# Weight splits of whole 128x2048 buffers, memory tokens kept in DRAM, and four sets of seven block products in the first feed-forward part

## The chip, the cores and the metric

The kernel runs on one core of one Trainium2 chip. The metric is the device time of one execution in microseconds (us). Before the change it is 1260.77 us, the median of 3 runs (1260.51 to 1260.87).

## What is computed

A trunk of two layers on 256 tokens of width 1024, all in fp32, batch 1. Memory is 256 further tokens, normalised once per layer with its own gain.

```python
for i in range(2):
    h = h + 0.5 * swiglu(rmsnorm(h, ffn1_norm[i]), ffn1_w_gate[i], ffn1_w_up[i], ffn1_w_down[i])
    hn = rmsnorm(h, mix_norm[i])
    h = h + (diff_attention(hn, ...) if i == 0 else ssd_mixer(hn, ...))
    h = h + memory_cross_attention(rmsnorm(h, xa_norm[i]), mem, xa_mem_norm[i], xa_w_q[i], xa_w_kv[i], xa_w_o[i])
    h = h + 0.5 * swiglu(rmsnorm(h, ffn2_norm[i]), ffn2_w_gate[i], ffn2_w_up[i], ffn2_w_down[i])
return rmsnorm(h, final_norm)

def swiglu(h, w_gate, w_up, w_down):      # hidden width 2816
    return (silu(h @ w_gate) * (h @ w_up)) @ w_down
```

## The kernel before

**Products.** TensorE (PE) multiplies fp32r operands. To keep fp32 accuracy, every operand is split into a rounded part (hi) and the rest (lo), and a product is three matmuls: hi by hi (line 262), hi by lo of the weights (263), lo by hi (264), function `mm3`.

**Weights.** A weight block of 4 x 128 rows and 512 columns is loaded with one DMA of 1 MB, issued on SyncE (SP), into a buffer of 128x2048 out of a pool of 8 (`wp`, tile `w`). A piece (`Gran`, lines 205 to 226) is half a block, 128x1024. It is split by a CAST on ScalarE (ACT, line 224, tile `whi`) and a subtract on VectorE (DVE, line 225, tile `wlo`), into two tiles of 128x1024 out of a pool of 4 (`hp`). `use` (line 236) splits two pieces (`AHEAD`) ahead of the one that PE multiplies. In the code a list of units says in which order the pieces come. `run_units` writes the first two units (gate 0 and up 0 of the first feed-forward part, FFN) by hand on PE, DVE, ACT and SP; the rest is put in order by a scheduler.

**FFN.** The hidden width 2816 is five blocks of 512 (0 to 4) and half a block (5). A block of gate and up by the plain way is 2 x 8 k-blocks x 2 halves of the tokens = 32 products of 128x512. `seven` (line 352) makes one of them in 28 products: the two weight matrices, cut into four blocks b11, b21 (of up), b12, b22 (of gate), are combined with sums of the activations so that seven block products with four products each do. Its operands are x1 = b11 + b12 (a sum on DVE, line 203), x2 = x1 + b22 (DVE too, into x1's buffer, after x1 has been split), x3 = b12 + b22 and x4 = x2 + b21 (accumulating DMAs on GpSimd, line 199). The order in a set is x1, b11, x2, b22, x3, b21, x4. The sums of activations are made on DVE (`sraw`, line 481, from `y`, line 560) and split as `s_hi` (ACT, 485) and `s_lo` (DVE, 486). Results in PSUM, tile `seven`, are copied and combined as `p` (lines 823 to 841).

**Hosts.** Ordinary pieces, of up 0, of the half block (`gateup`), and of the down projection (`out`), are put between the pieces of the sets: `share` places `counts[c][i]` of them ahead of the i-th piece of set c. A host piece is four products for each k-block pair: 2 k-blocks x 2 halves of the tokens. In the first FFN block 0 is done by hand, and half block 5 and block 1 by the plain way (`stream`), as hosts; blocks 2 to 4 are sets. In the other three FFNs blocks 1 to 4 are sets.

**Memory.** `mem_prep` transposes the normalised memory on PE and keeps it in SBUF as eight tiles `mem` of 128x256. The cross-attention reads them in `prep` (scaled and split as `mh`, `ml`, for the keys) and `mix` (scaled as `my`, for the values as sums).

Of the kernel before, what the change touches and what calls it, by code (L numbers as in the profile page):

```python
# [57 lines left out]
def trunk(ctx, tc, a, out):  # L58
# [146 lines left out]
    class Gran:  # L205


        def __init__(self, k0, nk, *parts, eng=None):
            self.k0, self.nk, self.parts, self.eng = k0, nk, parts, eng or nc.vector
            self.hi = None  # L210

        def split(self):
# [2 lines left out]
            hi = hp.tile([P, 1024], F32R, name="whi", tag="hi")
            lo = hp.tile([P, 1024], F32R, name="wlo", tag="lo")
            ncol = sum(n for _, _, n in self.parts)
            self.hi, self.lo = (t[:, :self.nk * ncol].rearrange("p (k c) -> p k c", c=ncol) for t in (hi, lo))
            o = 0
            for w, c0, n in self.parts:  # L220
                w.load()
                src = w.t[:, self.k0 - w.k0:self.k0 - w.k0 + self.nk, c0:c0 + n]
# [1 line left out]
                nc.scalar.copy(hv, src)  # L224
                self.eng.tensor_tensor(self.lo[:, :, o:o + n], src, hv.bitcast(F32), op=ALU.subtract)  # L225
# [462 lines left out]
    def mem_prep():  # L688
# [12 lines left out]
        def turn(j):  # L701
            ps = small_ps("tin")
            for t in range(2):
                nc.tensor.transpose(ps[:, t * P:(t + 1) * P], mnat[t][j // 4][:, (j % 4) * P:(j % 4 + 1) * P], ident)
            nc.scalar.copy(memt[j], ps[:, :S])
        for j in range(KT):
            pipe.after(6.0 + 1.0 * j, lambda j=j: turn(j))
# [349 lines left out]
    class MemKV:  # L1057


        def __init__(self, l):  # L1060
# [20 lines left out]

        def prep(self):
            self.x.clear()
            for j in range(KT):
                if j % 2 == 0:
                    mh, ml = slot("mh", F32R), slot("ml", F32R)
                xh, xl = (m[:, j % 2 * S:(j % 2 + 1) * S] for m in (mh, ml))
                split_act(xh, xl, memt[j], self.g[:, j:j + 1])
                self.x.append((xh, xl))
# [587 lines left out]
```

## Time and profile before

| what | value |
|---|---|
| median of 3 runs | 1260.77 us |
| the profiled execution | 1260.69 us |
| its span | 1258.9 us |
| busy: PE, DVE, ACT, POOL | 1248.6, 1056.7, 878.0, 161.7 us |
| granted PE clock, mean | 0.998 |
| splits of 128x1024 | 520 |
| weight reads from HBM and rest | 269.79 MB, mean 214 GB/s |

The span is what the profiler saw; 1.8 us of the execution lie around it. Busy times of engines overlap. PE's own busy time is modelled, so its waits are read from the distance between the starts of matmuls. In a row of the timeline the first column is the start in us from the span's beginning, the second the duration (of all that the row groups, "x2" is two of them), and in brackets stands how long the engine had been idle and what released it. A group's row ends with the busy time, the mean in ns of one, and the idle time ahead of it.

### The profile page before, as it was taken

Reading aid. Unit: us, or ns where it says so; the run is one execution under the profiler, and the core shown is the slowest. Engines: PE = TensorE matmul, PEld = TensorE weight load, DVE = VectorE, ACT = ScalarE, POOL = GpSimd, SP = SyncE. Lnnn points to the kernel's source line nnn. Section 1 sums busy time; section 2 is a strip of 40 time slices with the busy share of each in tenths; the row PEclk is TensorE's granted clock in tenths of the full one; section 3 lists DMA queues with packets and bytes.
Section 4 is the critical chain, followed back from the end, with each engine's and each line's share of the span. In section 5 each row is a group of like instructions: output and inputs, shape, how many; then the busy total and the mean of one; then the engine's idle time right before and its main releaser. Section 6 shows DMA issues by size and latency. Waiting matters only on the chain.

```text
span 1258.9 us, 18179 instructions
## 1 busy us (share of the span) xinstructions
PE 1248.6 (99%) x6751; PEld 1070.7 (85%) x6751; DVE 1056.7 (84%) x1451; ACT 878.0 (70%) x1395; POOL 161.7 (13%) x139
## 2 busy tenths in 40 slices
PE   9999999999999999999999999999999999999997
PEld 6887888788998888888888889999998898888886
DVE  6988867887787998988898976788899887899886
ACT  6676764676676876767776756777777775877673
POOL 1101002201101011101111000022232100011100
PEclk9999999999999999999999999999999999999999
DMA  9979975345776698985899966665634786489961
GB/s 335 281 205 283 319 240 183 118 144 150 209 226 168 168 264 270 267 268 167 219 273 265 289 228 214 205 186 168 201 135 135 189 245 177 159 235 276 261 215 34
DMA packets 158316, 269.79 MB, mean 214 GB/s; under 512 B 6890, under 2 KB 43411, under 8 KB 158227
## 3 DMA queue, kind: packets, MB, share of 16 engines
q1 hardware_dynamic: 137744, 229.75, 53.6%
q0 software_dynamic: 19744, 38.28, 17.8%
q8 instruction: 53, 0.87, 0.3%
q10 hardware_dynamic: 738, 0.59, 0.1%
q14 instruction: 37, 0.30, 0.1%
HBM read 267.52 MB, written 1.08 MB: 213 GB/s over the span
## 4 chain that ended last, share of the span: by engine, by line
PE 91%; DVE 4%; DMA 2%; ACT 1%; issue 1%; POOL 0%; POOLq 0%; DVEq 0%; ACTq 0%
PE out L263 9%; PE out L264 8%; PE out L262 8%; PE seven L264 8%; PE seven L263 8%; PE seven L262 8%; DVE wlo L225 2%; PE xs L264 2%; PE xs L262 1%; PE xs L263 1%; DMA w<-in_ffn_w_gate_dram 1%; PE up L263 1%; PE up L264 1%; PE up L262 1%; PE htp L854 1%; PE mk L262 1%
## 5 line engine op out<-in xcount | busy, mean ns | idle before, releaser
L225 DVE TENSOR_TENSOR wlo<-w,whi 128x1024 fp32r<-128x1024 f32 (+2 forms) x532 | 641.0, 1219 | 136.2 <-ACT whi L224 126.7
L224 ACT CAST whi<-w 128x1024 fp32r<-128x1024 f32 (+2 forms) x534 | 552.3, 1040 | 261.9 <-PE out L264 102.5
L262 PE MATMUL out<-whi,hid_hi 128*128 128x512 f32 x336 | 131.4, 394 | 0.5 <-ACT whi L224 0.5
L263 PE MATMUL out<-wlo,hid_hi 128*128 128x512 f32 x336 | 131.3, 391 | 0.4 <-DVE wlo L225 0.3
L264 PE MATMUL out<-whi,hid_lo 128*128 128x512 f32 x336 | 131.0, 390 | 0.0
L262 PE MATMUL seven<-whi,s_hi 128*128 128x512 f32 x272 | 107.7, 396 | 0.4 <-ACT p L823 0.4
L263 PE MATMUL seven<-wlo,s_hi 128*128 128x512 f32 x272 | 106.1, 390 | 0.0
L264 PE MATMUL seven<-whi,s_lo 128*128 128x512 f32 x272 | 106.1, 390 | 0.0
L203 DVE TENSOR_TENSOR w<-w 128x2048 f32<-128x2048 f32 x32 | 73.2, 2286 | 5.7 <-DMA w<-in_ffn_w_gate_dram 5.6
L199 POOL DMA_DIRECT2D w<-in_ffn_w_up_dram x30 | 36.5, 1241 | 310.5 <-DVE wlo L225 273.7
L263 PEld LDWEIGHTS out<-wlo,hid_hi 128*128 128x128 f32 x336 | 63.2, 188 | 14.7 <-DVE wlo L225 2.1
L262 PEld LDWEIGHTS out<-whi,hid_hi 128*128 128x128 f32 x336 | 63.0, 188 | 13.3 <-ACT whi L224 0.8
L264 PEld LDWEIGHTS out<-whi,hid_lo 128*128 128x128 f32 x336 | 63.1, 188 | 13.2
L262 PE MATMUL seven<-whi,xh 128*128 128x512 f32 x180 | 70.1, 389 | 0.0
L264 PE MATMUL seven<-whi,xl 128*128 128x512 f32 x180 | 70.0, 389 | 0.0
L263 PE MATMUL seven<-wlo,xh 128*128 128x512 f32 x180 | 70.0, 389 | 0.0
L199 POOL DMA_DIRECT2D w<-in_ffn_w_gate_dram x30 | 36.9, 1467 | 221.7 <-DVE w L203 76.2
L264 PEld LDWEIGHTS seven<-whi,s_lo 128*128 128x128 f32 x272 | 51.1, 188 | 10.8
L262 PEld LDWEIGHTS seven<-whi,s_hi 128*128 128x128 f32 x272 | 51.1, 188 | 10.5 <-ACT p L823 0.8
L263 PEld LDWEIGHTS seven<-wlo,s_hi 128*128 128x128 f32 x272 | 51.1, 188 | 9.7
L262 PEld LDWEIGHTS seven<-whi,xh 128*128 128x128 f32 x180 | 33.8, 188 | 7.1
L263 PEld LDWEIGHTS seven<-wlo,xh 128*128 128x128 f32 x180 | 33.8, 188 | 7.1
(398 smaller groups left out, 3018.4 us busy)
## 6 DMA issues: line engine op xcount, KB each, us to landing
w<-in_ffn_w_up_dram SPq DMA_DIRECT2D x40, 1024.0 KB, 7.2
w<-in_ffn_w_down_dram SPq DMA_DIRECT2D x40, 1024.0 KB, 8.6
w<-in_ffn_w_gate_dram SPq DMA_DIRECT2D x38, 1024.0 KB, 7.1
w<-in_ssd_w_in_dram SPq DMA_DIRECT2D x24, 1024.0 KB, 5.4
w<-in_xa_w_kv_dram SPq DMA_DIRECT2D x16, 1024.0 KB, 5.1
w<-in_ffn_w_gate_dram POOLq DMA_DIRECT2D x30, 512.0 KB, 9.1
w<-in_ffn_w_up_dram POOLq DMA_DIRECT2D x30, 512.0 KB, 7.4
w<-in_da_w_in_dram SPq DMA_DIRECT2D x12, 1024.0 KB, 5.2
```

The costliest lines, as they stand in the source:

```text
L199: nc.gpsimd.dma_start(self.t[:, k:k + 2, :], w.src[r0:r0 + 2 * P, w.c0:w.c0 + w.n] .rearrange("(k p) c -> p k c", p=P), accum_op=ALU.add)
L203: nc.vector.tensor_tensor(self.t, self.l.t, w.t, op=ALU.add)
L224: nc.scalar.copy(hv, src)
L225: self.eng.tensor_tensor(self.lo[:, :, o:o + n], src, hv.bitcast(F32), op=ALU.subtract)
L262: nc.tensor.matmul(o, lhsT=lh, rhs=rh, start=start, stop=False, skip_group_check=onto)
L263: nc.tensor.matmul(o, lhsT=lh, rhs=rl, start=False, stop=False, skip_group_check=onto)
L264: nc.tensor.matmul(o, lhsT=ll, rhs=rh, start=False, stop=stop, skip_group_check=onto)
L854: nc.tensor.transpose(tp[:, j, t * P:(t + 1) * P], us[t][:, (i + j) * P:(i + j + 1) * P], ident)
```

## The change

Four things are changed.

1. Splits. Two neighbouring pieces of one weight block (k-blocks 0 and 1, 2 and 3 of a buffer, 512 columns) are now split together: one CAST and one subtract of 128x2048. A new class `Group` decides which pieces belong together; other pieces are still split one by one, into halves of a tile. `hp` has 3 tiles of 128x2048 instead of 4 of 128x1024.
2. Memory. The transposed memory lies in DRAM. Four tiles `mt` of 128x512 are written from ACT's queue, and each `prep` and `mix` first fetches four tiles of 256 KB back, on ACT's queue too, and works some 4 to 5 us later by the code's own plan.
3. The weight pool `wp` has 7 buffers instead of 8.
4. The first FFN makes block 1 as a fourth set of seven, and `counts` are even numbers everywhere, so that the two pieces of a block stay together.

```diff
-    wp = ctx.enter_context(tc.tile_pool(name="wp", bufs=8))
-    hp = ctx.enter_context(tc.tile_pool(name="hp", bufs=4))
+    wp = ctx.enter_context(tc.tile_pool(name="wp", bufs=7))
+    hp = ctx.enter_context(tc.tile_pool(name="hp", bufs=3))
...
+    class Group:
...
+        def take(self, g, unit):
+            a = self.gs[-1]
+            if len(self.gs) == 1 and a.whole(g):
+                self.merged = True
...
+        def split(self, g):
+            if self.t is None:
+                self.t = [hp.tile([P, 2048], F32R, name=n, tag=n) for n in ("whi", "wlo")]
+            if self.merged:
...
+                src = w.t[:, a.k0 - w.k0:a.k0 - w.k0 + 4, :]
+                nc.scalar.copy(hi, src)
+                nc.vector.tensor_tensor(lo, src, hi.bitcast(F32), op=ALU.subtract)
...
-    memt = [const.tile([P, S], F32, name=f"mem{j}") for j in range(KT)]
+    memt = dram.tile([P, KT * S], F32, name="memt")
...
+            mt = slot("mt")
+            nc.scalar.copy(v2(mt), ps)
+            nc.scalar.dma_start(memt[:, 512 * i:512 * i + 512], mt)
...
-        five, six = [1, 0, 1, 0, 2, 0, 1], [1, 1, 1, 0, 2, 0, 1]
...
-            n = half + stream([(wg, 512, 512)], norm, "gate", gate_fin(1)) + stream([(wu, 512, 512)], norm, "up", up_fin(1))
-            counts = {2: [5, 1, 1, 0, 2, 1, 1], 3: [1, 1, 1, 1, 2, 1, 1], 4: [1, 1, 1, 0, 2, 1, 1]}
+            n = half
+            counts = {1: [0, 0, 2, 0, 2, 0, 0], 2: [2, 0, 2, 0, 2, 0, 0], 3: [0, 0, 2, 0, 2, 0, 0], 4: [0, 0, 2, 0, 2, 0, 0]}
...
-            counts = {1: six, 2: five, 3: six, 4: five}
+            counts = {c: [2, 0, 2, 0, 2, 0, 0] for c in (1, 2, 3)}
+            counts[4] = [0, 0, 2, 0, 2, 0, 0]
...
+        def fetch(self):
+            y = [slot("my") for _ in range(KT // 2)]
+            for p in range(KT // 2):
+                nc.scalar.dma_start(y[p], memt[:, 512 * p:512 * p + 512])
+            return y
...
         def mix(self):
-            y = [slot("my") for _ in range(KT // 2)]
+            y = self.fetch()
...
-                pipe.after(1.4 * p, lambda p=p: full(p))
-            combine(y, self.s, [7.0 + 1.6 * i for i in range(8)])
+                pipe.after(5.0 + 1.4 * p, lambda p=p: full(p))
+            combine(y, self.s, [12.0 + 1.6 * i for i in range(8)])
...
         def prep(self):
             self.x.clear()
...
+            y = self.fetch()
...
+            for p in range(KT // 2):
+                pipe.after(4.0 + 1.0 * p, lambda p=p: cut(p))
```

How the order of the instructions moves. First DVE at the start, from the first up block on; each name is a tile (`wlo` the lo part of weights, `y` and `sraw` activations, `w<-w` the sum of two weight buffers). Before:

```order
L225 TENSOR_TENSOR wlo<-w,whi 128x1024 x2
L560 TENSOR_TENSOR y<-xh,xl 128x256 x2
L225 TENSOR_TENSOR wlo<-w,whi 128x1024
L560 TENSOR_TENSOR y<-xh,xl 128x256 x2
L225 TENSOR_TENSOR wlo<-w,whi 128x1024
L560 TENSOR_TENSOR y<-xh,xl 128x256 x4
L1268 TENSOR_SCALAR dskh<-vec 128x32
L225 TENSOR_TENSOR wlo<-w,whi 128x1024
L481 TENSOR_TENSOR sraw<-y 128x256 x2
L486 TENSOR_TENSOR s_lo<-sraw,s_hi 128x512
```

And now, at the same place on DVE:

```order
L253 TENSOR_TENSOR wlo<-w,whi 128x2048
L605 TENSOR_TENSOR y<-xh,xl 128x256 x2
L253 TENSOR_TENSOR wlo<-w,whi 128x2048
L605 TENSOR_TENSOR y<-xh,xl 128x256 x6
L1328 TENSOR_SCALAR dskh<-vec 128x32
L203 TENSOR_TENSOR w<-w 128x2048
L253 TENSOR_TENSOR wlo<-w,whi 128x2048
L526 TENSOR_TENSOR sraw<-y 128x256 x2
L203 TENSOR_TENSOR w<-w 128x2048
L531 TENSOR_TENSOR s_lo<-sraw,s_hi 128x512
```

The two subtracts of up 0 that each served half a buffer are one; the gateup split that stood ahead of `sraw` has been replaced by the sum x1 and its split, and the sum x2 stands ahead of `s_lo`. On PE, at the end of up 0 (`pcol` are two small transposes of parameters), before:

```order
L263 MATMUL up<-wlo,xh 128x512
L264 MATMUL up<-whi,xl 128x512
L673 MATMUL pcol<-ident,rows_99 128x128 x2
L262 MATMUL gateup<-whi,xh 128x512
L263 MATMUL gateup<-wlo,xh 128x512
L264 MATMUL gateup<-whi,xl 128x512
```

And now on PE:

```order
L308 MATMUL up<-wlo,xh 128x512
L309 MATMUL up<-whi,xl 128x512
L718 MATMUL pcol<-ident,rows_99 128x128 x2
L307 MATMUL seven<-whi,s_hi 128x512
L308 MATMUL seven<-wlo,s_hi 128x512
L307 MATMUL seven<-whi,xh 128x512
L309 MATMUL seven<-whi,s_lo 128x512
```

PE goes from up 0 straight to the first set, with b11's first product (`whi,xh`) slipped in ahead of the first matmul that needs `s_lo`. Last, DVE in the first FFN where one set ends and the next begins (`p` are results of a set, the sums `w<-w` x1 or x2, `hid_lo` the hidden activations). Before, between the third and the fourth block:

```order
L841 SCALAR_TENSOR_TENSOR p_1133<-seven,rcol,p_1133 128x512
L225 TENSOR_TENSOR wlo<-w,whi 128x1024 x3
L841 SCALAR_TENSOR_TENSOR p_1010<-seven,rcol,p_1010 128x512
L225 TENSOR_TENSOR wlo<-w,whi 128x1024
L203 TENSOR_TENSOR w<-w 128x2048
L225 TENSOR_TENSOR wlo<-w,whi 128x1024
```

And now, between the second and the third:

```order
L890 SCALAR_TENSOR_TENSOR p_894<-seven,rcol,p_894 128x512
L253 TENSOR_TENSOR wlo<-w,whi 128x2048
L890 SCALAR_TENSOR_TENSOR p_802<-seven,rcol,p_802 128x512
L766 TENSOR_TENSOR lampr<-lqk 128x128
L203 TENSOR_TENSOR w<-w 128x2048
L767 TENSOR_REDUCE lam<-lampr 128x2
L253 TENSOR_TENSOR wlo<-w,whi 128x2048 x2
```

The sum x2 (`w<-w`) stands behind the split of the new set's b11 and ahead of the split of the first host, and both splits are whole buffers.

More of the change, by code (lines that the diff above doesn't have):

```diff
@@ L210, in __init__, with size, whole @@
             self.hi = None
-        def split(self):
-            if self.hi is not None:
+        def size(self):
+            return self.nk * sum(n for _, _, n in self.parts)
+        def whole(self, other):
+            w, c0, n = self.parts[0]
+            return (self.parts == other.parts and len(self.parts) == 1 and (c0, n) == (0, 512)
+                    and self.nk == other.nk == 2 and other.k0 == self.k0 + 2)
+        def split(self):
+            if self.hi is None:
+                self.group.split(self)
@@ new lines, in trunk, with __init__ @@
+    class Group:
+        def __init__(self, g):
+            self.gs, self.n = [g], g.size()
+            self.merged = False
+            self.t = None
+        def take(self, g, unit):
+            a = self.gs[-1]
+            if len(self.gs) == 1 and a.whole(g):
+                self.merged = True
+            elif unit != a.unit or self.merged or self.n + g.size() > 2048 or a.parts[0][2] == g.parts[0][2] == 512 and a.nk > 1:
+                return False
+            self.gs.append(g)
+            self.n += g.size()
+            return True
+        def split(self, g):
+            if self.t is None:
+                self.t = [hp.tile([P, 2048], F32R, name=n, tag=n) for n in ("whi", "wlo")]
+            if self.merged:
+                a, b = self.gs
+                w = a.parts[0][0]
+                w.load()
+                hi, lo = (t.rearrange("p (k c) -> p k c", c=512) for t in self.t)
+                src = w.t[:, a.k0 - w.k0:a.k0 - w.k0 + 4, :]
+                nc.scalar.copy(hi, src)
+                nc.vector.tensor_tensor(lo, src, hi.bitcast(F32), op=ALU.subtract)
+                for x, k in ((a, 0), (b, 2)):
+                    x.hi, x.lo = hi[:, k:k + 2, :], lo[:, k:k + 2, :]
@@ L214, in split @@
                 return
[L215 to L218, printed above, removed]
+            ncol = sum(n for _, _, n in g.parts)
+            o = sum(x.size() for x in self.gs[:self.gs.index(g)])
+            g.hi, g.lo = (t[:, o:o + g.size()].rearrange("p (k c) -> p k c", c=ncol) for t in self.t)
@@ L219, in split @@
             o = 0
-            for w, c0, n in self.parts:
+            for w, c0, n in g.parts:
                 w.load()
-                src = w.t[:, self.k0 - w.k0:self.k0 - w.k0 + self.nk, c0:c0 + n]
-                hv = self.hi[:, :, o:o + n]
+                src = w.t[:, g.k0 - w.k0:g.k0 - w.k0 + g.nk, c0:c0 + n]
+                hv = g.hi[:, :, o:o + n]
                 nc.scalar.copy(hv, src)
-                self.eng.tensor_tensor(self.lo[:, :, o:o + n], src, hv.bitcast(F32), op=ALU.subtract)
+                g.eng.tensor_tensor(g.lo[:, :, o:o + n], src, hv.bitcast(F32), op=ALU.subtract)
@@ L243, in run_units @@
     def run_units():
-        for gs, _ in units:
+        for i, (gs, _) in enumerate(units):
             for g in gs:
-                g.at = len(grans)
+                g.at, g.unit = len(grans), i
+                if not grans or not grans[-1].group.take(g, i):
+                    g.group = Group(g)
+                else:
+                    g.group = grans[-1].group
                 grans.append(g)
@@ L699, in mem_prep, with turn @@
                 nc.scalar.activation(mnat[t][c], mnat[t][c], AF.Copy, scale=mcol[:, t:t + 1])
[L701 to L707, printed above, removed]
+        def turn(i):
+            ps = v2(small_ps("tin"))
+            for j in (2 * i, 2 * i + 1):
+                for t in range(2):
+                    nc.tensor.transpose(ps[:, j % 2, t * P:(t + 1) * P], mnat[t][j // 4][:, (j % 4) * P:(j % 4 + 1) * P],
+                                        ident)
+            mt = slot("mt")
+            nc.scalar.copy(v2(mt), ps)
+            nc.scalar.dma_start(memt[:, 512 * i:512 * i + 512], mt)
+        for i in range(KT // 2):
+            pipe.after(6.0 + 2.0 * i, lambda i=i: turn(i))
     def mem_stage():
@@ L1083, in prep, with cut @@
             self.x.clear()
[L1084 to L1089, printed above, removed]
+            y = self.fetch()
+            def cut(p):
+                mh, ml = slot("mh", F32R), slot("ml", F32R)
+                for j in range(2):
+                    k = 2 * p + j
+                    xh, xl = v2(mh)[:, j, :], v2(ml)[:, j, :]
+                    split_act(xh, xl, v2(y[p])[:, j, :], self.g[:, k:k + 1])
+                    self.x.append((xh, xl))
+            for p in range(KT // 2):
+                pipe.after(4.0 + 1.0 * p, lambda p=p: cut(p))
         def k_units(self, then=None, cs=(0, 2)):
```

2 lines of the change are left out of this document (1 added, 1 removed).

## The prediction, made before the changed kernel was timed

> **What bounds the kernel now.** I read the page first: the busy times, the slices and the chain that ended last.
>
> ```profile
> span 1258.9 us, 18179 instructions
> PE 1248.6 (99%) x6751; PEld 1070.7 (85%) x6751; DVE 1056.7 (84%) x1451; ACT 878.0 (70%) x1395; POOL 161.7 (13%) x139
> PE   9999999999999999999999999999999999999997
> DVE  6988867887787998988898976788899887899886
> DMA  9979975345776698985899966665634786489961
> PE 91%; DVE 4%; DMA 2%; ACT 1%; issue 1%; POOL 0%; POOLq 0%; DVEq 0%; ACTq 0%
> PE out L263 9%; PE out L264 8%; PE out L262 8%; PE seven L264 8%; PE seven L263 8%; PE seven L262 8%; DVE wlo L225 2%; PE xs L264 2%; PE xs L262 1%; PE xs L263 1%; DMA w<-in_ffn_w_gate_dram 1%; PE up L263 1%; PE up L264 1%; PE up L262 1%; P
> ```
>
> PE is 99% busy and carries 91% of the chain. So the time is the number of matmuls, and whatever makes PE wait. DVE has 84%, and its share of the chain (4%) lies mostly in the first feed-forward part (FFN): its tenths are highest in the slices 2 to 4, and DMA is full in the slices 1 and 2 (31.5 us each). Next the groups, for the price of a split, and four stretches of the timeline.
>
> ```profile
> L225 DVE TENSOR_TENSOR wlo<-w,whi 128x1024 fp32r<-128x1024 f32 x520 | 633.9, 1233 | 131.0 <-ACT whi L224 121.6 <-DMA E<-scr 1.6
> L224 ACT CAST whi<-w 128x1024 fp32r<-128x1024 f32 x520 | 544.7, 1053 | 260.9 <-PE out L264 102.5 <-PE seven L264 43.3 <-PE gateup L264 15.9
> L203 DVE TENSOR_TENSOR w<-w 128x2048 f32<-128x2048 f32 x32 | 73.2, 2286 | 5.7 <-DMA w<-in_ffn_w_gate_dram 5.6
> ```
>
> A 128x1024 subtract takes 1233 ns; the one DVE operation on a whole buffer, the sum of two weight blocks, takes 2286. A whole-buffer subtract has the sum's shape (three fp32 operands of 128x2048), so I price it at 2.29 us. PE around the start of the first up block (columns: start, duration, both in us):
>
> ```profile
> 19.25 0.39 PE L262 MATMUL up<-whi,xh 128*128 128x512 f32 x1
> 19.76 0.50 PE L263 MATMUL up<-wlo,xh 128*128 128x512 f32 x1
> ...
> 30.32 0.40 PE L264 MATMUL up<-whi,xl 128*128 128x512 f32 x1
> 30.55 0.38 PE L673 MATMUL pcol<-ident,rows 128*128 128x128 f32 x2
> 30.69 0.47 PE L262 MATMUL gateup<-whi,xh 128*128 128x512 f32 x1
> 31.01 0.39 PE L263 MATMUL gateup<-wlo,xh 128*128 128x512 f32 x1
> 31.24 0.40 PE L264 MATMUL gateup<-whi,xl 128*128 128x512 f32 x1
> ```
>
> Matmuls overlap, so what counts is start to start: 31.24 less 31.01 is 0.23, and the 46 steps from 19.76 to 30.32 make 0.23 each. A product (hi by hi, hi by lo, lo by hi) is three of these, 0.69 us.
>
> **The matmuls saved.** The hidden block 1 of the first FFN was 32 products (gate and up, 16 each) and becomes a set of seven pieces with four products each, 28. That is 12 matmuls by 0.23: **-2.76 us**, on PE itself. This term is certain.
>
> **The first up block, cut whole.** ACT and DVE there:
>
> ```profile
> 17.41 3.89 ACT L224 CAST whi<-w 128x1024 fp32r<-128x1024 f32 x4
> ...
> 18.48 2.45 DVE L225 TENSOR_TENSOR wlo<-w,whi 128x1024 fp32r<-128x1024 f32 x2 [0.58 <-ACT whi L224]
> 20.86 0.84 DVE L560 TENSOR_TENSOR y<-xh,xl 128x256 f32<-128x256 f32 x2
> ```
>
> Four casts take 3.89, so a whole buffer (two of them) takes some 1.95: from 17.41 to 19.4. The subtract can only then begin, and ends at 19.4 + 2.29 = 21.7. Before, the first half was through at 19.7 and PE's second up matmul started at 19.76. Now it starts at 21.7: **+1.94 us**. Nothing hides it, since the order on PE, ACT and DVE at that place stays and PE has no other work. The lower bound would be 0.97 (a cast of twice the size at the price of one), the upper 2.3.
>
> [...]
>
> **The first set of seven, right behind up 0.** Before, the gateup pieces stood there, which need only one split each. Now the first product needs the sum x1 of two buffers, its split, and a mixed activation (s). The rows for the parts:
>
> ```profile
> 27.13 0.75 DVE L481 TENSOR_TENSOR sraw<-y 128x256 f32<-128x256 f32 x2
> 28.56 0.69 DVE L486 TENSOR_TENSOR s_lo<-sraw,s_hi 128x512 fp32r<-128x512 f32 x1 [0.69 <-ACT s_hi L485]
> ...
> 27.91 0.62 ACT L485 CAST s_hi<-sraw 128x512 fp32r<-128x512 f32 x1 [2.28 <-DVE sraw L481]
> ...
> 23.41 1.06 ACT L224 CAST whi<-w 128x1024 fp32r<-128x1024 f32 x1 [2.11 <-DMA w<-in_ffn_w_up_dram]
> 24.36 1.27 ACT L787 ACTIVATE gs<-gate,rcol 128x512 f32<-128x512 f32 x2
> ...
> GB/s 392 385 381 388 388 392 362 319 295 268 324 349 353 354 360 347 347 346 349 360 370 388 378 381 381 392 385 395 388 378 388 388 392 385 378 395 388 388 385 378
> ```
>
> The last line is the DMA rate from 13 to 36 us, some 385 GB/s at its end, so a buffer of 1 MB follows the one before by 2.7 us. The first buffer behind up 0 landed at 23.4 (ACT waited for it), the second then at 26.1 to 26.3. I walk DVE in its new order. The subtract of up's second buffer 22.5 to 24.7; six operations y at 0.35 and dskh to 26.9; sum x1 to 29.1 (both buffers are there); ACT's cast to 31.1; the subtract to 33.4; sraw to 34.1; s_hi on ACT (behind the cast of b11, which ends at 34.4) to 34.9. PE has ended up 0 at 30.55 + 1.94 = 32.5 and the two small pcol at 32.65, and waits to 34.9: 2.25. DVE goes on with the sum x2 (2.2, to 36.3) and only then s_lo, to 36.95: PE waits some 1.45 for its third kind of matmul. The subtract of b11 comes behind s work and gs, at 41.7: 1.15. The first gateup piece: 0.45. Together **+5.30 us**. The bounds: 0.75 (only the wait for x1's own split, 33.4 less 32.65), and 5.3 with another 2.3 if one more whole operation is late.
>
> **A stall of before that should go.** PE in the first FFN at 94 to 97 us:
>
> ```profile
> 94.05 0.61 PE L262 MATMUL out<-whi,hid_hi 128*128 128x512 f32 x2
> 95.02 0.49 PE L262 MATMUL seven<-whi,s_hi 128*128 128x512 f32 x1 [0.35 <-ACT p L823]
> 95.96 0.73 PE L262 MATMUL out<-whi,hid_hi 128*128 128x512 f32 x2 [0.45 <-ACT whi L224]
> 96.98 0.50 PE L263 MATMUL out<-wlo,hid_hi 128*128 128x512 f32 x1 [0.29 <-DVE wlo L225]
> 97.31 0.40 PE L264 MATMUL out<-whi,hid_lo 128*128 128x512 f32 x1
> ```
>
> Six steps should take 1.38 and took 3.26. DVE had run late there among the small operations of the rotary angles. In the new order these stand between whole buffers with host pieces near, and the stretch differs throughout: **-1.88 us** (bounds -1.9 and 0).
>
> **From one set to the next.** The new counts put hosts (ordinary pieces) only ahead of a set's third and fifth piece, and in some sets ahead of the first. Where the next set has none at its front, five pieces of seven follow each other: x3, b21, x4, then x1 and b11. PE needs 5 x 12 x 0.23 = 13.8 us for them. DVE's rows:
>
> ```profile
> 67.10 2.29 DVE L203 TENSOR_TENSOR w<-w 128x2048 f32<-128x2048 f32 x1 [1.97 <-DMA w<-in_ffn_w_gate_dram]
> 69.31 3.49 DVE L225 TENSOR_TENSOR wlo<-w,whi 128x1024 fp32r<-128x1024 f32 x3
> 72.72 0.68 DVE L835 TENSOR_TENSOR p<-p,seven 128x512 f32<-128x512 f32 x1
> 73.32 1.22 DVE L225 TENSOR_TENSOR wlo<-w,whi 128x1024 fp32r<-128x1024 f32 x1
> ...
> 77.41 0.74 DVE L841 SCALAR_TENSOR_TENSOR p<-seven,rcol,p 128x512 f32<-128x512 f32 x1
> 78.07 1.22 DVE L225 TENSOR_TENSOR wlo<-w,whi 128x1024 fp32r<-128x1024 f32 x1
> ```
>
> Start to start a whole buffer takes 2.21, the two kinds of p operation 0.60 and 0.66. In that time DVE has five splits, the sum x2 ahead of the host's split, and four p operations: 6 x 2.21 + 2.52 = 15.8. It loses 2.0 us, less the lead that it has. The lead is between nothing and one piece (2.2); between these ends I choose 1.2 from set 2 to 3 (0.8 lost), 0.7 from 3 to 4, where set 4's own sum x1 stands earlier and eats lead (1.3 lost), and 0.3 lost from 1 to 2, which has hosts at its front. In the other three FFNs there is one such place each, behind sets with more hosts, so with most of the lead: 0.3 each, 0.9. Together **+3.30 us**, between 0 and 5 x 2.0 + 0.3 = 10.3.
>
> **Memory in DRAM.** Four writes and twenty reads of 256 KB are issued on ACT's queue.
>
> ```profile
> L685 SPq DMA_DIRECT2D mnat<-in_mem_dram x4: 358/414/590, 125.4 to 127.1; - x4
> ...
> E<-scr SPq DMA_DIRECT2D x16, 256.0 KB, 5.9
> ...
> mnat<-in_mem_dram SPq DMA_DIRECT2D x4, 256.0 KB, 9.6
> ```
>
> Twenty-four issues of 0.414 are 9.9 us on ACT, which is 70% busy; its idle time hides them, and if it didn't they would cost up to 9.9. The wait is worse: ACT works in order, and the casts of weights stand behind an operation on a buffer that hasn't landed. The code plans 4 to 5 us from fetch to use; loads of that size took 5.9 and 9.6. PE holds up to two split pieces meanwhile (some 5.4 us). I take **0**, with 0 to 6 in the range.
>
> The larger splits also relieve DVE: 218 pairs by 2 x 1233 - 2286 = 180 ns, some 39 us of its busy time, most of it beside a busy PE and worth nothing there. The weight pool of seven buffers instead of eight delays loads; the DMA share behind 63 us has room, so I take 0 (0 to 2).
>
> **The sum.** The profiled execution took 1260.69 us (span 1258.9 and 1.8 around it), 0.08 under the median of 1260.77. 1260.69 - 2.76 + 1.94 + 5.30 - 1.88 + 3.30 = **1266.6 us**.
>
> **Rivals.** *Faster: DVE's relief reaches PE.* Splits lie with 2% of the chain on DVE, 25 us; 180 of 2466 ns less is 1.8. If the first set costs only its x1 split (0.75) and no transition loses anything, 1260.69 - 2.76 + 1.94 + 0.75 - 1.88 - 1.8 = 1256.9. It decides (under 1258.2) from the point where the first set's waits stay under 2.0 us with transitions at nothing. For it: DVE is 84% busy and in the first 100 us the tightest engine behind PE. Against it: s_lo stands behind the sum x2 in DVE's order. Chance 0.16. [...]
>
> *No change.* Half of the first set's waits (2.6) and no loss between sets: 1260.69 - 2.76 + 1.94 + 2.6 - 1.88 = 1260.6. Chance 0.14.
>
> *Memory.* One or two of the five fetches land 3 us later than PE's lead covers: 1266.6 + 3 to 6, say 1271.1. For it: 9.6 us to landing in one row. Against it: DMA is 30 to 40% busy in the slices 8 and 9 (220 to 283 us), where the first of them lie. Chance 0.10.
>
> *The change doesn't do what it says:* the new order has 218 whole splits and 90 of the old size, so it does, for the larger part; no chance of its own.
>
> **How the numbers follow.** The forecast has 0.60, the memory case 0.10 and both are slower; 0.2% (2.5 us) is about what a measurement of this kernel can tell from no change. So faster 0.16, same 0.14, slower 0.70. The range takes in no change, half of the faster case, and on the other side memory or transitions at their worse half: 1258.0 to 1272.5. The likeliest case's own range is 1263.3 to 1271.
>
> **What would show it.** In the profile of the changed kernel: PE's second up matmul at some 21.7; a gap of about 2 us ahead of the first seven, then waits for s_lo and for the split of b11; no stall at 94 to 97; gaps of about 1 us where a set starts without hosts, with DVE the releaser; ACT's waits for memory short. The forecast is wrong if the first seven follows up 0 with less than 1 us, if waits for DMA on the memory buffers appear, or if DVE is the releaser nowhere behind 50 us.

## The result, and the profile after

The changed kernel takes 1297.63 us (median of 4 runs, 1296.87 to 1297.84) against 1260.67 before: 1.0292 times the time, with an interval of 1.0274 to 1.0310. It is 37 us slower. The direction was forecast, the size was not: 1266.6 was said, with a range to 1272.5.

The page of the changed kernel, some of the lines that answer to those of before:

```profile
span 1295.9 us, 17549 instructions
PE 1261.7 (97%) x6739; PEld 1074.3 (83%) x6739; DVE 1051.3 (81%) x1243; ACT 847.1 (65%) x1182; POOL 173.5 (13%) x143
...
PE 72%; DVE 11%; issue 6%; ACT 5%; DMA 5%; POOL 1%; POOLq 0%; DVEq 0%; ACTq 0%; SPq 0%
```

PE has the 12 matmuls less that were counted, and DVE and ACT are less busy than before (81% for 84, 65% for 70). Yet PE's share of the chain has fallen from 91 to 72%, and DVE, ACT and DMA stand in for it. Neither DVE nor ACT has more work than before, so the time must lie in waits. The groups say what the whole splits cost by themselves:

```profile
L253 DVE TENSOR_TENSOR wlo<-w,whi 128x2048 fp32r<-128x2048 f32 x218 | 499.4, 2295 | 120.9 <-ACT whi L252 119.5 <-PE seven L308 1.0
L252 ACT CAST whi<-w 128x2048 fp32r<-128x2048 f32 x218 | 416.9, 1913 | 199.0 <-PE out L309 67.7 <-PE seven L309 50.9 <-DVE w L203 15.0
L307 PE MATMUL seven<-whi,s_hi 128*128 128x512 f32 x288 | 116.1, 403 | 14.9 <-DVE p L879 14.7
```

A whole subtract takes 2295 ns (priced at 2.29 us), a whole cast 1913 (1.95). The third row is the find: PE waited 14.7 us for an operation `p` on DVE, which it never did before. The view of the waits gives how often, and what DVE itself waited for:

```profile
DVE w L203 <- DMA w<-in_ffn_w_gate_dram: 28.1, 14, 5.4
PE seven L307 <- DVE p L879: 14.7, 4, 4.3
```

Four waits of up to 4.3 us, and DVE's sums of two weight buffers (`w`, line 203) waited 28.1 us for loads, where it was 5.6 before. One of the four places, on DVE, then on PE (start, duration, both in us), then the DMA issue:

```profile
442.83 2.29 DVE L253 TENSOR_TENSOR wlo<-w,whi 128x2048 fp32r<-128x2048 f32 x1 [0.49 <-ACT whi L252]
...
454.80 2.29 DVE L203 TENSOR_TENSOR w<-w 128x2048 f32<-128x2048 f32 x1 [4.78 <-DMA w<-in_ffn_w_gate_dram]
457.00 0.69 DVE L907 TENSOR_TENSOR hid_lo<-htp,hid_hi 128x512 fp32r<-128x512 f32 x1
457.61 2.28 DVE L253 TENSOR_TENSOR wlo<-w,whi 128x2048 fp32r<-128x2048 f32 x1
459.80 0.69 DVE L907 TENSOR_TENSOR hid_lo<-htp,hid_hi 128x512 fp32r<-128x512 f32 x1
460.40 0.68 DVE L879 TENSOR_TENSOR p<-p,seven 128x512 f32<-128x512 f32 x1
...
457.13 0.39 PE L309 MATMUL gateup<-whi,xl 128*128 128x512 f32 x1
461.23 0.47 PE L307 MATMUL seven<-whi,s_hi 128*128 128x512 f32 x1 [3.71 <-DVE p L879]
...
445.15 0.37 SPq L161 DMA_DIRECT2D w<-in_ffn_w_gate_dram  x1
```

The subtract that ends at 445.13 frees a weight buffer. At 445.15 the load of the next set's second block (b12) is issued into it, and it lands at 454.7, 9.6 us later. DVE has that set's sum x1 next in its order and stands still for 4.78 us. Behind it in the queue are a `hid_lo`, a split, another `hid_lo` and `p`, none of which needs that load. PE needs `p`, since the product x3 is added to the bank that `p` reads. So PE stands from 457.4 to 461.2. The load's time and what follows the wait are seen in the stretches (columns: the window, busy time and instructions of PE, PEld, DVE, ACT and POOL, the granted PE clock, the DMA share, GB/s):

```profile
448.00:450.00 2.00, 2.00 (x15) 1.75 (x14) 2.00 (x1) 1.50 (x1) 0.00 (x0) 1.00 0.99 197
450.00:452.00 2.00, 2.00 (x11) 1.64 (x10) 0.02 (x1) 0.89 (x2) 0.00 (x0) 1.00 1.10 262
...
462.00:464.00 2.00, 2.00 (x7) 1.58 (x6) 1.62 (x2) 1.64 (x1) 0.00 (x0) 0.55 1.11 189
464.00:466.00 2.00, 2.00 (x7) 1.59 (x6) 2.00 (x2) 0.15 (x1) 0.00 (x0) 0.59 1.05 250
466.00:468.00 2.00, 2.00 (x11) 1.65 (x10) 0.77 (x2) 2.00 (x2) 0.00 (x0) 1.00 1.05 333
```

While the load is under way the DMA share is 0.99 and 1.10, so it finds no idle DMA engines. Two accumulating loads, issued on GpSimd from 442.7 on, run in the same stretch; that they delay it was not tested. After PE's wait the granted clock is 0.55 and 0.59 for 4 us, and 7 matmuls fall into 2 us instead of 11.

By stages (from the first matmul of one stage to the first of the next, in the PE timelines), as differences to the kernel before. The runs other than "after" are explained below; FFN 2 to 4 are the other three feed-forward parts.

| stage, us before | after | pool of 7 alone | counts and fourth set alone | after with halves | after with order edge |
|---|---|---|---|---|---|
| FFN 1, to the attention's q: 190.4 | +9.9 | +1.6 | +5.1 | +8.3 | +5.2 |
| attention: 84.8 | +1.8 | 0.0 | +1.1 | +0.9 | +1.8 |
| its cross-attention: 130.2 | +0.3 | +0.1 | 0.0 | 0.0 | +0.5 |
| FFN 2: 175.8 | +6.1 | +3.8 | -0.2 | +1.5 | +0.5 |
| FFN 3: 174.9 | +6.9 | +3.4 | -0.2 | +3.6 | +1.6 |
| SSD: 240.9 | +5.1 | 0.0 | 0.0 | +1.1 | +4.0 |
| its cross-attention: 79.9 | +0.5 | -0.3 | -0.3 | -0.4 | +0.9 |
| FFN 4 to the end: 182.0 | +6.3 | +2.0 | -0.4 | +0.8 | +0.5 |

FFN 2 to 4, where 0.9 us was forecast, hold 19.3 of the 37 us.

### The profile page after: what moved, and what is told of

It reads as the page before. It is cut to its first block, busy times and chain, and to the rows that moved or that the text cites. A ratio compares the mean times of both kernels' runs of the same rounds, so it can differ in the third digit from the quotient of the medians.

```text
span 1295.9 us, 17549 instructions
## 1 busy us (share of the span) xinstructions
PE 1261.7 (97%) x6739; PEld 1074.3 (83%) x6739; DVE 1051.3 (81%) x1243; ACT 847.1 (65%) x1182; POOL 173.5 (13%) x143
## 4 chain that ended last, share of the span: by engine, by line
PE 72%; DVE 11%; issue 6%; ACT 5%; DMA 5%; POOL 1%; POOLq 0%; DVEq 0%; ACTq 0%; SPq 0%
PE out L308 9%; PE out L309 8%; PE out L307 8%; PE seven L307 6%; PE seven L308 6%; PE seven L309 6%; DVE wlo L253 5%; DMA w<-in_ffn_w_gate_dram 4%; ACT whi L252 2%; PE mk L307 1%; PE mk L309 1%; PE mk L308 1%; PE xq L307 1%; PE xq L309 1%; PE xq L308 1%
## 5 line engine op out<-in xcount | busy, mean ns | idle before, releaser
L253 DVE TENSOR_TENSOR wlo<-w,whi 128x2048 fp32r<-128x2048 f32 x218 | 499.4, 2295 | 120.9 <-ACT whi L252 119.5
L252 ACT CAST whi<-w 128x2048 fp32r<-128x2048 f32 x218 | 416.9, 1913 | 199.0 <-PE out L309 67.7
L266 DVE TENSOR_TENSOR wlo<-w,whi 128x1024 fp32r<-128x1024 f32 (+2 forms) x102 | 119.2, 1178 | 27.1 <-ACT whi L265 26.5
L265 ACT CAST whi<-w 128x1024 fp32r<-128x1024 f32 (+2 forms) x104 | 100.7, 983 | 50.8 <-PE out L309 11.8
L307 PE MATMUL seven<-whi,s_hi 128*128 128x512 f32 x288 | 116.1, 403 | 14.9 <-DVE p L879 14.7
L309 PE MATMUL seven<-whi,s_lo 128*128 128x512 f32 x288 | 115.1, 400 | 1.2 <-DVE s_lo L531 1.2
L308 PE MATMUL seven<-wlo,s_hi 128*128 128x512 f32 x288 | 115.0, 399 | 0.0
L203 DVE TENSOR_TENSOR w<-w 128x2048 f32<-128x2048 f32 x34 | 77.8, 2289 | 30.2 <-DMA w<-in_ffn_w_gate_dram 28.1
L307 PE MATMUL seven<-whi,xh 128*128 128x512 f32 x192 | 75.8, 395 | 1.1 <-DVE p L884 1.1
L308 PE MATMUL seven<-wlo,xh 128*128 128x512 f32 x192 | 75.3, 392 | 0.7 <-DVE wlo L253 0.7
L309 PE MATMUL seven<-whi,xl 128*128 128x512 f32 x192 | 74.9, 390 | 0.0
```

The costliest lines, as they stand in the source:

```text
L203: nc.vector.tensor_tensor(self.t, self.l.t, w.t, op=ALU.add)
L252: nc.scalar.copy(hi, src)
L253: nc.vector.tensor_tensor(lo, src, hi.bitcast(F32), op=ALU.subtract)
L266: g.eng.tensor_tensor(g.lo[:, :, o:o + n], src, hv.bitcast(F32), op=ALU.subtract)
L307: nc.tensor.matmul(o, lhsT=lh, rhs=rh, start=start, stop=False, skip_group_check=onto)
L308: nc.tensor.matmul(o, lhsT=lh, rhs=rl, start=False, stop=False, skip_group_check=onto)
```

## The experiments

Three theories for the 37 us were put down first. **A, the pool:** with seven buffers loads come late. **B, the grain:** whole splits are too coarse. **C, the counts:** hosts stand in other places, and the next sum gets ahead of `p`. After the first four runs C was narrowed to **D, the order on DVE:** a sum that waits for a load stands ahead of work that PE needs.

**The pool back to eight**, in the changed kernel:

```diff
-    wp = ... bufs=7     sp = ... bufs=28
+    wp = ... bufs=8     sp = ... bufs=24
```

> The changed kernel with eight weight buffers again (the room comes from four of the 28 activation slots). Theory A (the pool): with seven buffers the load of the next set's second block is issued one freed buffer later, the sum on DVE waits for it, and the split and the p operation that PE needs stand behind that sum. Then the four PE waits for p (14.7 us together) and the slow clock behind them go: about 1278 us. Theory B (the whole splits): buffers are freed and work is done too coarsely; nothing changes here, 1297. Theory C (the new counts: hosts no longer stand ahead of a set's last piece, and the scheduler puts the next sum ahead of the p operation): the waits become shorter but stay, about 1290.

Measured: 1293.13 us (ratio 1.0259, interval 1.0242 to 1.0276), 4.5 less than the changed kernel. PE's waits for `p` stay, but fall from 14.7 to 7.0 us, and three of the four move to the next set; DVE there, in FFN 2:

```profile
485.51 2.29 DVE L203 TENSOR_TENSOR w<-w 128x2048 f32<-128x2048 f32 x1 [3.51 <-DMA w<-in_ffn_w_gate_dram]
487.72 2.28 DVE L253 TENSOR_TENSOR wlo<-w,whi 128x2048 fp32r<-128x2048 f32 x1
489.92 0.68 DVE L879 TENSOR_TENSOR p<-p,seven 128x512 f32<-128x512 f32 x1
```

The same picture as at 454: the sum waits, and a split and `p` stand behind it. At the place of before, the first set of FFN 2 to 4, the sum stands ahead of `p` here too (439.7 and 448.8 us in FFN 2), but its load has landed, and PE doesn't wait. The SSD stage is 6.7 us longer here than in the changed kernel, which may be the four slots taken away, so this run doesn't price the pool well. It refutes A as the whole cause, and shows that the late load is a part of it.

**The pool of seven in the kernel before**, nothing else:

```diff
-    wp = ctx.enter_context(tc.tile_pool(name="wp", bufs=8))
+    wp = ctx.enter_context(tc.tile_pool(name="wp", bufs=7))
```

> The kernel before with seven weight buffers, nothing else. Theory A: its own sums on DVE now wait for loads, 10 to 20 us more, 1270 to 1280. Theories B and C: the buffer is worth at most 2 us, 1261 to 1263.

Measured: 1271.25 us (ratio 1.0082, interval 1.0067 to 1.0097). So the buffer has a price of 10.4 us by itself, where I had taken 0 to 2. It lies in FFN 2 to 4 (9.2 of it), and it is a wait of the same kind, with splits behind the sum instead of `p`:

```profile
479.65 2.29 DVE L203 TENSOR_TENSOR w<-w 128x2048 f32<-128x2048 f32 x1 [3.07 <-DMA w<-in_ffn_w_gate_dram]
481.86 3.49 DVE L225 TENSOR_TENSOR wlo<-w,whi 128x1024 fp32r<-128x1024 f32 x3
...
483.13 0.50 PE L263 MATMUL seven<-wlo,xh 128*128 128x512 f32 x1 [0.99 <-DVE wlo L225]
```

**Halves in the changed kernel**: the class `Gran` of before, with its own cast and subtract of 128x1024, in the kernel after.

```diff
-    hp ... bufs=3, whi and wlo of 128x2048, one split for two pieces
+    hp ... bufs=4, whi and wlo of 128x1024, one split for one piece
```

> The changed kernel with splits of 128x1024 as before (four tile pairs of that size), with the new counts, memory in DRAM and seven weight buffers. Theory A: the waits for p stay, only the first up block's 2 us and part of the start go: 1290 to 1296. Theory B: most of the loss goes: 1262 to 1268. Theory C: as A, about 1290.

Measured: 1276.58 us (ratio 1.0128, interval 1.0113 to 1.0143). With halves 21 of the 37 us are gone; that is between what A and B expected, and looked like B. But DVE's order is another one here:

```profile
447.89 1.28 DVE L862 TENSOR_TENSOR hid_lo<-htp,hid_hi 128x512 fp32r<-128x512 f32 x2
449.09 1.22 DVE L225 TENSOR_TENSOR wlo<-w,whi 128x1024 fp32r<-128x1024 f32 x1
450.22 0.68 DVE L834 TENSOR_TENSOR p<-p,seven 128x512 f32<-128x512 f32 x1
450.84 1.23 DVE L225 TENSOR_TENSOR wlo<-w,whi 128x1024 fp32r<-128x1024 f32 x1
452.72 2.29 DVE L203 TENSOR_TENSOR w<-w 128x2048 f32<-128x2048 f32 x1 [0.65 <-DMA w<-in_ffn_w_gate_dram]
```

With halves the scheduler has put `p` ahead of the sum at this place. The sum starts late, at 452.72, and waits for its load as well, but with nothing urgent behind it. So two things had changed with the splits, the grain and the order.

**The new counts and the fourth set in the kernel before**: halves, eight buffers, memory in SBUF.

```diff
-            n = half + stream(gate 1) + stream(up 1)
-            counts = {2: [5, 1, 1, 0, 2, 1, 1], 3: [1, 1, 1, 1, 2, 1, 1], 4: [1, 1, 1, 0, 2, 1, 1]}
+            n = half
+            counts = {1: [0, 0, 2, 0, 2, 0, 0], 2: [2, 0, 2, 0, 2, 0, 0], ...}
```

> The kernel before with the new counts and the fourth set in the first feed-forward part only: halves, eight weight buffers, memory in SBUF. Theory A: no waits for p; only the start of the first part costs some 5 us against 2.8 saved: 1261 to 1265. Theory B: the same, 1258 to 1265. Theory C: the four waits are there in part: 1272 to 1290.

Measured: 1264.89 us (ratio 1.0032, interval 1.0020 to 1.0044). PE has no wait for `p` here: C by itself is refuted, and so are the counts as a cause in FFN 2 to 4 (-0.2, -0.2, -0.4). The order is there all the same: in FFN 2 the sum starts at 442.54, after 0.35 us of waiting for its load, and `p` stands behind it at 449.36. With the load in time, the order cost nothing here. The time is lost in FFN 1 (+5.1 in the table) and in the attention (+1.1).

**The order edge**, the run that decides between B and D. It adds no instruction to the changed kernel; it only forbids the scheduler to put a sum x1 ahead of the last `p` operation that subtracts:

```diff
+                    if self.into is None and behind:
+                        st.enter_context(tc.issue_after(behind[-1].ins))
                     nc.vector.tensor_tensor(self.t, self.l.t, w.t, op=ALU.add)
...
-                    v.tensor_tensor(us[0], t[2], b[3], op=ALU.subtract)
+                    behind.append(v.tensor_tensor(us[0], t[2], b[3], op=ALU.subtract))
```

> The changed kernel; the only edit is that DVE's sum x1 of a next set may not be put ahead of the p operation that ends the reading of a bank in the set before (an order edge, no other instruction added). Theory D (order in DVE's queue): the sum waits for a late load and holds the splits and the p operation behind it; then the waits of PE for p (14.7 us, 4 places) and the slow clock behind them go, 1276 to 1282. Theory A (the pool alone: the loads come late and something must wait for them): the wait only moves to the next split, 1290 to 1297. Theory B (the whole splits are too coarse for PE): the same, 1290 to 1297.

Measured: 1276.10 us (ratio 1.0119, interval 1.0104 to 1.0134), 21.5 less than the changed kernel. D is borne out: with whole splits, seven buffers and the new counts all in place, one edge brings back as much as the halves did. DVE and the waits in it:

```profile
445.83 2.29 DVE L258 TENSOR_TENSOR wlo<-w,whi 128x2048 fp32r<-128x2048 f32 x1 [0.43 <-ACT whi L257]
448.04 1.28 DVE L912 TENSOR_TENSOR hid_lo<-htp,hid_hi 128x512 fp32r<-128x512 f32 x2
449.24 0.68 DVE L884 TENSOR_TENSOR p<-p,seven 128x512 f32<-128x512 f32 x1
449.84 2.29 DVE L208 TENSOR_TENSOR w<-w 128x2048 f32<-128x2048 f32 x1
...
DVE w L208 <- DMA w<-in_ffn_w_gate_dram: 8.9, 8, 1.8
```

The four operations that stood behind the sum (a split, two `hid_lo`, `p`) fill the time of the load, and at 449.84 the sum waits for nothing. The sums' waits for loads of gate weights fall from 28.1 to 8.9 us, PE waits for this `p` no more, and the clock's mean is 0.997 instead of 0.989. By the table the four feed-forward parts get back 21.4 us. The shares of the chain hardly move (PE 73%, DVE 11%), so they hadn't pointed at these 21 us.

**Two operations for each whole split**, same groups and tiles:

```diff
-                nc.scalar.copy(hi, src)
-                nc.vector.tensor_tensor(lo, src, hi.bitcast(F32), op=ALU.subtract)
+                for k in (0, 2):
+                    nc.scalar.copy(hi[:, k:k + 2, :], src[:, k:k + 2, :])
+                    nc.vector.tensor_tensor(lo[:, k:k + 2, :], src[:, k:k + 2, :], ..., op=ALU.subtract)
```

> The changed kernel with the same groups, tiles and counts, but each whole split done as two casts and two subtracts of 128x1024. Theory B (one operation on a whole buffer is too coarse): as with halves throughout, 1275 to 1282. Theory D: the time goes with the order on DVE; where the sum x1 still stands ahead of the p operation the waits stay, 1288 to 1298.

Measured: 1279.56 us (ratio 1.0144, interval 1.0129 to 1.0159), in the window of B and under that of D. The sum stands ahead of `p` here too, in this row 5.7 us ahead of it:

```profile
1128.14 2.29 DVE L203 TENSOR_TENSOR w<-w 128x2048 f32<-128x2048 f32 x1 [4.80 <-DMA w<-in_ffn_w_gate_dram]
...
1133.81 0.68 DVE L880 TENSOR_TENSOR p<-p,seven 128x512 f32<-128x512 f32 x1
```

PE still waits for `p` four times, but 9.0 us in all instead of 14.7: its steps at the three such places of FFN 2 to 4 are 1.2, 1.4 and 3.1 us too long, where the changed kernel has 3.9, 3.3 and 4.5, and behind the first two the clock stays at 1.00. So the price of the wrong order depends on the grain and the moment too; it isn't one number.

D's window was missed, and that counts against D as the full account of the 21 us. Whole splits with the sum ahead of `p` take 1297.6 us. With the edge alone it is 1276.1 us, with operations of half the size alone 1279.6 (this run), and with halves and `p` first at the place shown 1276.6. Either remedy brings back 18 us or more, and the other then adds little. So the loss needs the order and the whole splits together, and, by the runs with eight buffers, a load that comes late.

**Memory in DRAM alone**, in the kernel before:

```diff
-    memt = [const.tile([P, S], F32, name=f"mem{j}") for j in range(KT)]
+    memt = dram.tile([P, KT * S], F32, name="memt")
```

> The kernel before with memory in DRAM and nothing else. All theories: ACT's extra issues and waits are mostly hidden, 0 to 2 us, 1261 to 1263. If ACT's waits for the fetches reach PE: 1264 to 1270.

Measured: 1261.41 us (ratio 1.0003, interval 0.9993 to 1.0013). No difference, as forecast.

**The gateup pieces ahead of the fourth set**, in the kernel before with four sets in FFN 1:

```diff
+            counts = {1: [4, 1, 1, 0, 1, 0, 1], 2: [1, 0, 1, 0, 1, 0, 0], 3: [1, 0, 1, 0, 1, 0, 1], 4: [1, 0, 1, 0, 1, 0, 0]}
```

> The kernel before (halves, eight buffers, memory in SBUF) with block 1 of the first part as a fourth set, but all four gateup pieces ahead of that set, and one host at a time later. If the fourth set costs only because nothing stands between up 0 and its first sum: the 2.8 us of saved matmuls show and part of the 2 us at 94 to 97, 1256 to 1259. If DVE is short of time throughout the first part: 1261 to 1266, with the waits further on.

Measured: 1262.08 us (ratio 1.0007, interval 0.9997 to 1.0016). 2.8 us better than the fourth set right behind up 0, and level with before: by its trace FFN 1 is only 0.2 us shorter than before, in spite of the matmuls saved, and the attention 1.3 longer.

**The first up buffer in halves**, on top of the order edge:

```diff
-            if len(self.gs) == 1 and a.whole(g):
+            if len(self.gs) == 1 and a.whole(g) and not (unit == 1 and a.k0 == 0):
```

> The kernel with the order edge, and the first buffer of the first up block split in halves as before; all else whole. If nothing hides the whole split there (the 1.94 us of the prediction), PE's 2.1 us wait goes and the time falls by about 2: 1274. If the first set, which starts right behind, waits for its own sum anyway, the wait only moves there: 1276.

Measured: 1276.27 us (ratio 1.0121, interval 1.0105 to 1.0136): no gain over the edge alone. The 2 us wait in the up block is gone, and PE waits in front of the first set instead:

```profile
34.30 0.80 PE L312 MATMUL seven<-whi,s_hi 128*128 128x512 f32 x1 [3.54 <-ACT s_hi L535]
```

**And the gateup pieces first** on top of that. In this kernel the fifth piece of a set has no host ahead of it, so by the code's own timing two of its products are added to a bank before `p` reads it: the sets' results are wrong, the work is the same.

```diff
+            counts = {1: [4, 0, 2, 0, 0, 0, 0], 2: [2, 0, 2, 0, 0, 0, 0], 3: [2, 0, 2, 0, 0, 0, 0], 4: [2, 0, 2, 0, 0, 0, 0]}
```

> As the kernel with the first up buffer in halves, and the four gateup pieces stand ahead of the fourth set, so that the first set of seven has time for its sum and split. If the first set's place costs what the profile shows in the first 50 us (6.5 us more than before, 2 of them in the up block): 1270 to 1272. If DVE stays behind throughout the first part: 1273 to 1276.

Measured: 1279.33 us (ratio 1.0141, interval 1.0127 to 1.0155), outside both windows. Taking the fifth piece's host away puts new waits behind `s_lo` matmuls in every set of FFN 1, so this doesn't tell what the place of the gateup pieces is worth.

**The order edge with eight buffers**, room made by two lo tiles instead of three:

```diff
-[hp.tile([P, 2048], F32R, name=n, tag=n) for n in ("whi", "wlo")]
+[hp.tile([P, 2048], F32R, name=n, tag=n, bufs=b) for n, b in (("whi", 3), ("wlo", 2))]
```

> The kernel with the order edge and eight weight buffers; the room comes from the lo tiles, two instead of three. If the seven buffers still cost 10 us with whole splits (as they do with halves): about 1266. If the order edge already hides the late loads: 1274 to 1277; if two lo tiles are too few: slower than 1277.

Measured: 1283.19 us (ratio 1.0172, interval 1.0157 to 1.0187). In the window for too few lo tiles: FFN 2 to 4 are 4.1, 3.9 and 4.7 us longer than before, and PE waits for lo parts eleven times in `seven` and `out`, 7.8 us in all. Inconclusive on the pool.

**A try for a version that beats both**: the kernel before, four sets, six hosts ahead of the first, and the order edge.

```diff
+            counts = {1: [6, 0, 1, 0, 1, 0, 0], 2: [1, 0, 1, 0, 1, 0, 0], 3: [1, 0, 1, 0, 1, 0, 1], 4: [1, 0, 1, 0, 1, 0, 0]}
```

> A try for a version that beats both: the kernel before with the fourth set in the first part, the four gateup and two down pieces ahead of it, and the order edge. If what is lost in the first part comes from a sum that stands too early: the 2.8 us of saved matmuls show, 1257.5 to 1259.5. If DVE has no time to spare there: 1260 to 1263.

Measured: 1259.86 us (ratio 0.9985, interval 0.9977 to 0.9994). It is the fastest of all, 1 to 3 us ahead of the kernel before, and lies between the two windows: part of the 2.8 us arrives.

**Whole splits only in the feed-forward parts**, with the edge:

```diff
-            if len(self.gs) == 1 and a.whole(g):
+            if len(self.gs) == 1 and a.whole(g) and a.big and g.big:     # big: made in a feed-forward part
```

> The kernel with the order edge; whole splits only in the feed-forward parts (170 of 218), halves in attention, SSD and cross-attention. The edge left 15 us over the kernel before, of which the stages between the feed-forward parts hold 7.2 by the spans (1.8 in the attention, 4.1 in the SSD, 1.3 elsewhere). If they come from the whole splits there: 1270 to 1272. If from memory in DRAM, the smaller pool or the shifted order: 1275 to 1277.

Measured: 1274.62 us (ratio 1.0101, interval 1.0084 to 1.0118), against 1276.10 with the edge alone, and between the two windows. The attention stage gets back 0.9 of its 1.8 us, but the SSD stage is 6.2 us longer than before, not 4.0. So most of the loss there isn't the whole splits of that stage.

**Block 1 by the plain way**, with the edge:

```diff
-            counts = {1: [0, 0, 2, 0, 2, 0, 0], 2: [2, 0, 2, 0, 2, 0, 0], ...}
+            counts = {2: [6, 0, 2, 0, 2, 0, 2], 3: [2, 0, 2, 0, 2, 0, 2], 4: [2, 0, 2, 0, 2, 0, 0]}
```

> The kernel with the order edge and block 1 of the first feed-forward part by the plain way again, as hosts in pairs; all else as with the edge. The first part is 5.2 us longer than before with the edge. If the fourth set is what costs there: 5 us less, 1270 to 1272 (its 2.8 us of matmuls come back in). If the whole splits and the pool cost there anyway: 1274 to 1278.

Measured: 1277.85 us (ratio 1.0125, interval 1.0110 to 1.0141). It lies in the second window, and FFN 1 is 7.4 us longer than before instead of 5.2. But some 5 us of that are one wait that the run with the edge alone doesn't have: PE stands idle for 3.50 us at 127.52, for a split, and the clock is 0.63 and 0.52 for 4 us behind it. So the run doesn't tell what the fourth set costs.

## Why the prediction was wrong, step by step

**The matmuls saved**: right. PE has 6739 instead of 6751.

**The first up block (+1.94)**: right as a wait, but it is no cost of its own. PE in the changed kernel:

```profile
19.61 0.50 PE L307 MATMUL up<-whi,xh 128*128 128x512 f32 x1
21.94 0.80 PE L308 MATMUL up<-wlo,xh 128*128 128x512 f32 x1 [1.82 <-DVE wlo L253]
...
25.43 0.40 PE L307 MATMUL up<-whi,xh 128*128 128x512 f32 x1
...
34.85 0.50 PE L307 MATMUL seven<-whi,s_hi 128*128 128x512 f32 x1
...
37.00 0.50 PE L309 MATMUL seven<-whi,s_lo 128*128 128x512 f32 x1 [1.19 <-DVE s_lo L531]
41.65 0.50 PE L308 MATMUL seven<-wlo,xh 128*128 128x512 f32 x1 [0.74 <-DVE wlo L253]
```

The second up matmul starts at 21.94 (21.7 was said). I didn't reckon with the slow clock behind the wait (0.50 in the window from 22 to 24 us, 0.67 in the next): from 21.94 to 25.43 eight steps take 3.49 us, 1.65 more than at 0.23. PE finishes up later by that, which is most of the time that the first set would have made it wait. So the gap of 2 us ahead of the first seven, one of the signs named, isn't there: it follows the small pcol of 34.32 with less than 1 us. In the run with halves there, PE's clock is 1.00 from 20 to 32 us, and PE waits 3.54 us for the first set.

**The first set (+5.30)**: right in place. The walk along DVE's order gave 34.9, 36.95 and 41.7 for the first seven, its lo matmul and b11; they start at 34.85, 37.00 and 41.65. DVE sets this stretch, so what PE loses earlier is not lost again, and the two terms hold as one sum only.

**The stall at 94 to 97 (-1.88)**: wrong. In its place stands a wait for `p`, from 97.97 to 101.95, of the kind found above. The terms of FFN 1 made +5.0 in all; it is +9.9, and with the edge +5.2. That this comes so near is in part luck, since the terms in it weren't right one by one.

**From one set to the next (+3.30), and the weight pool (0)**: here the prediction failed. I priced DVE's own work at these places and took nothing for the pool because the DMA share behind 63 us has room. For these parts that was a misreading: in the DMA row shown with the prediction the slices of FFN 2 and 3 (14 to 24) are mostly 8 and 9, and in the changed kernel the share is about 1 while the late load is under way. That load isn't issued before a subtract frees a buffer, and took 9.6 us to land. And I didn't look at what stands behind a waiting sum. In the order of the changed kernel the sum x1 stands ahead of `p` at the first set of FFN 2, in the order of before behind it; that could be read without a trace. The order alone wouldn't have told the price: at the next set the kernel before has the sum ahead of `p` too, and there it waits for nothing.

```profile
469.27 2.29 DVE L203 TENSOR_TENSOR w<-w 128x2048 f32<-128x2048 f32 x1
...
474.35 0.68 DVE L830 TENSOR_TENSOR p<-p,seven 128x512 f32<-128x512 f32 x1
```

FFN 2 to 4 lose 19.3 us where 0.9 was put down. With the edge they lose 2.6.

**Memory (0)**: right, 1.0003 (0.9993 to 1.0013).

**The rivals**: none of them named this mechanism. The faster one rested on DVE's relief. DVE's busy time did fall, by 5.4 us in all; its splits by the two pages from 641.0 to 618.6, 22.4 us where 39 was worked out. It brought nothing that shows: what counted was what stood in the queue, and when.

**What stays open.** Shown are: the order on DVE (21.5 us by the edge alone), a price of the pool with halves (10.4), of counts and the fourth set (4.0), of memory (none). These don't add: the 21.5 belong to this order with whole splits and seven buffers, and with the edge, seven buffers cost FFN 2 to 4 only 2.6 us against 9.2 with halves. Of the 15 us that the edge leaves, 5.2 lie in FFN 1 and 4.0 in the SSD stage. In the first, a walk accounts for the start. In the second the trace with the edge shows the places: PE falls 1.6 us behind the kernel before ahead of `acs`, 0.7 ahead of `tx` and 1.6 ahead of `pcb`. At the first of them DVE, then PE:

```profile
792.25 1.22 DVE L271 TENSOR_TENSOR wlo<-w,whi 128x1024 fp32r<-128x1024 f32 x1
793.75 1.22 DVE L271 TENSOR_TENSOR wlo<-w,whi 128x1024 fp32r<-128x1024 f32 x1
796.95 0.22 DVE L1330 SCALAR_TENSOR_TENSOR av<-dt,nega 128x64 f32<-128x64 f32 x1
797.28 0.41 PE L1340 MATMUL acs<-av,cst 128*128 128x64 f32 x2 [1.81 <-issue]
```

`acs` needs `av`, and two splits stand between the reciprocal at 791.27 and `av`, where the kernel before has one and PE waits 0.23 us. So this too looks like an order on DVE, which no run tests. Which of the four changes led to it no run tells: neither memory, nor the pool, nor the counts, nor the whole splits there have it alone. No run has the whole splits alone either, with eight buffers, the old counts and memory in SBUF.

## What to carry to other kernels

Before you price an engine's work, read its order: on DVE here, a sum that waited 4.78 us for its load held a split, two `hid_lo` and `p` behind it, and one edge that lets the urgent work pass was worth 21 us. Where the load was in time the order cost nothing (-0.2, -0.2 and -0.4 us in FFN 2 to 4 with the new counts in the kernel before), so ask of each such instruction when its load can start. One buffer fewer in a pool cost 10.4 us in the kernel before: look at when the buffer becomes free, add the time to landing (9.6 us at the place shown), and read the DMA share of that stretch (0.99 and 1.10 there), not of the whole run. And don't add the waits of PE along a stretch that another engine sets: walk that engine's order, and take the end.

## What the runs showed of the hardware

PE's granted clock fell to 0.50 behind a wait of 1.82 us. The changed kernel at the first up block, where PE stood idle up to 21.94:

```profile
20.00:22.00 2.00, 0.17 (x2) 0.06 (x1) 2.00 (x2) 1.35 (x1) 0.00 (x0) 0.97 1.04 393
22.00:24.00 2.00, 2.00 (x5) 1.63 (x6) 2.00 (x3) 0.00 (x0) 0.00 (x0) 0.50 1.05 392
24.00:26.00 2.00, 2.00 (x8) 1.59 (x7) 2.00 (x5) 0.00 (x0) 0.00 (x0) 0.67 1.08 393
```

The clock is 0.50, matmuls start 0.43 us apart, and some 3.5 us later (the step from 25.43 on) they are 0.23 to 0.24 us apart again, with a clock of 1.00 from 26 to 28 us. In the kernel before with seven buffers PE stands idle for 1.50 us up to 120.41, and its clock stays at 1.00, to 126 us at least:

```profile
120.00:122.00 2.00, 1.59 (x6) 1.05 (x6) 2.00 (x3) 1.01 (x2) 2.00 (x2) 1.00 0.31 37
```

The length of the wait alone didn't decide. Ahead of `acs` in the SSD stage PE stands idle for 1.82 us in the changed kernel and for 1.81 us with the order edge. Behind it the clock is 0.50 from 814 to 816 us in the first (upper row; PE starts again at 812.81), and 1.00 up to 799 us in the second (lower row; from 797.28):

```profile
814.00:816.00 2.00, 2.00 (x10) 2.00 (x10) 0.41 (x1) 0.17 (x1) 0.00 (x0) 0.50 0.63 227
...
797.00:799.00 2.00, 1.72 (x13) 1.51 (x14) 1.20 (x5) 0.46 (x2) 0.00 (x0) 1.00 1.06 385
```

What decides was not tested. By the windows behind the wait at 457 us (0.55 and 0.59 for 2 us each) that wait cost its own length, 3.71 us, and an estimated 1.7 us of slow matmuls. The four waits for `p`, 14.7 us, make some 21.5 us with 1.7 each, an estimate from this one place, and the edge brings back 21.5.
